# A long-convolution block on one core: the 16-point transforms as 32x32 blocks, and mirrored filter rows in one matmul

## The chip, the cores and the metric

The kernel runs on one core of a Trainium2 chip. The metric is device time in microseconds of one execution. The median of three runs of the kernel before is 1267.15 us.

## The reference

A block with a hyena branch and a pooling branch, for one sequence of L = 2048 positions and 1024 channels. The part that the change touches is the convolution of the 512 hyena channels with filters as long as the sequence, through Fourier transforms, twice over (`HYENA_ORDER` = 2).

```python
def hyena_filters(L, w1, b1, w2, b2, w3, b3, freq, w_proj):
    ...
    h = (h @ w_proj).reshape(L, HYENA_ORDER, N_DIRECTIONS, HYENA_WIDTH)
    ...
    return h * decay[:, None, None, :]

def two_sided_spectrum(h):
    ...
    k_full = jnp.concatenate([k_fwd, jnp.zeros_like(k_fwd[:1]), k_bwd[:0:-1]], axis=0)
    return jnp.fft.rfft(k_full, n=2 * L, axis=0)

def fft_conv(u, k_f, d):
    ...
    u_f = jnp.fft.rfft(uf, n=2 * L, axis=1)
    y = jnp.fft.irfft(u_f * k_f[None], n=2 * L, axis=1)[:, :L]
    return (y + uf * d.astype(jnp.float32)).astype(u.dtype)

def hybrid_layer(x, ...):
    h = rms_norm(x, pre_g)
    p = jnp.einsum('bld,dk->blk', h, w_in)
    hy = short_conv(p[..., :HYENA_IN], conv_w, conv_b)
    v = hy[..., :HYENA_WIDTH]
    gates = (hy[..., HYENA_WIDTH:2 * HYENA_WIDTH], hy[..., 2 * HYENA_WIDTH:])
    ...
    k_f = two_sided_spectrum(hyena_filters(L, ...))
    y = v
    for o in range(HYENA_ORDER):
        y = gates[o] * fft_conv(y, k_f[:, o], hyena_d[o])
    y_h = rms_norm(y * jax.nn.silu(z_h), norm_h_g)
    y_p = rms_norm(multiscale_pool(u_p, pool_w, pool_scale) * jax.nn.silu(z_p), norm_p_g)
    out = jnp.einsum('blk,kd->bld', jnp.concatenate([y_h, y_p], axis=-1), w_out)
    return x + rms_norm(out, post_g)
```

## The kernel before

**Stages.** From 0 to 404 us of the span the input projection and the pooling branch run, from 404 to 599 us the projection in natural layout (L553 to L555), from 599 to 644 us the head of the convolution phase, from 644 to 1120 us eight loops `gloop(o, q)` (o is the order 0 or 1, q one of four blocks of 128 channels), and from 1120 to 1264 us the tail with the output projection.

**The transform.** A sequence of 2048 points is transformed in two stages: 128-point transforms over the partitions (`s1` for the signal, `s1k` for the filter, with the tables f1 and f1s), a rearrangement by 32x32 transposes on DVE (`trans`, L623), and 16-point transforms in `gloop`. The transformed signal lies in BS[q], the transformed filter in BK[o, q]; both are f32.

**A gloop** has eight steps m. `kern(m)` (L720 to L725) transforms the filter by four f32 matmuls of 128x128 against `gf`, a table with four blocks on the diagonal of each 128x128 square; ACT copies the two halves of the partitions to kk (L722, L723), and two DMAs on SP's queue write them again to the other half, since the complex product needs each value on both halves. `mult(m)` (L732 to L739) transforms the signal by four matmuls against `gf`; ACT makes the swapped copy xs (L734, L735), DVE multiplies the product px by kk (L737), POOL multiplies xs by kk (L738), DVE adds both (L739). `back(m)` (L746, L747) transforms back by four matmuls against `gi`, and ACT copies the result to BS[q]. The order of the closures is kern(m+1), mult(m), back(m-1). pk, px and pc have a PSUM bank each (tags pk, x, c, one buffer each); f has a bank, k and s two each.

**Order of the work.** `run(main, *sides)` mixes the closures of side lists among those of a gloop by their place in the list: the filter of a later gloop (`pre_k`: `gen` makes filter rows, `s1k` transforms them), the signal of a later gloop (`post0`, `post1`, `pre_s`) and tiles of the output projection of the pooling branch (`fills`, L815 to L838). The calls of `run`, first `gloop(0, 0)`, then (0, 1), (1, 0), (1, 1), (0, 2), (0, 3), (1, 2), (1, 3), stand in L849 to L875. The framework orders the instructions of each engine from there and sets the waits; each engine executes in that order. `gen(j)` has two halves h, each with two rows n2 and for each the two directions dr: eight matmuls of 128 columns in f32r (L669), the high and the low part of the weights in turn.

## Time and profile before

| | us |
|---|---|
| median of three runs (1261.64 to 1273.34) | 1267.15 |
| profiled execution, its own time | 1265.96 |
| its span | 1264.0 |
| head of the convolution phase, 599 to 644 | 45.0 |
| eight gloops, 644 to 1120, 64 steps | 476.0 |
| tail, 1120 to 1264 | 144.0 |

PE is TensorE's matmuls, PEld its weight loads, DVE VectorE, ACT ScalarE, POOL GpSimd, SP SyncE. Busy times are shares of a stretch; a matmul's end is modelled. An f32 matmul shows as two rows of PE and two of PEld, so a count of 512 stands for 256 matmuls of the program. A row of a timeline gives start, length, engine, line, operation, tiles out<-in, shape, and in brackets the idle time before it with what ended it.

### The profile page before, as it was taken

The numbers are of one execution on the slowest core, as the hardware profiler recorded it, in microseconds if no ns is written. First come the engines' busy times: TensorE is split into PE (matmuls) and PEld (weight loads), VectorE is DVE, ScalarE is ACT, GpSimd is POOL, SyncE is SP. The second block draws the span as 40 slices with busy tenths as digits, with TensorE's granted clock in tenths as the row PEclk, the third lists the DMA queues.
The fourth block names the chain that finished last, engine by engine and source line by source line (L and its number), as shares of the span: only waits on it lengthen the run. The fifth ranks groups of instructions, "written<-read, shape, count | busy, mean of one in ns | idle before, by whom it ended". The sixth has DMA issues, their size and how long they took to land. (4 is left out here: it accounts for less than half of the span.)

```text
span 1264.0 us, 19047 instructions
## 1 busy us (share of the span) xinstructions
PE 1174.8 (93%) x7064; PEld 1012.7 (80%) x7064; DVE 823.8 (65%) x1343; ACT 480.5 (38%) x795; POOL 488.4 (39%) x436
## 2 busy tenths in 40 slices
PE   7999999999999999899899899999998999899984
PEld 5788888787788999899677788887887888877763
DVE  6965538436536658566464777766567777658987
ACT  7612112111112111200236566655556666844221
POOL 3212021504452568557222445422325354334534
PEclk9899999999999999999899999999999999999987
DMA  7224122223242253423795435456564447465574
GB/s 256 86 59 126 35 84 83 84 78 113 90 146 79 86 152 97 134 77 138 266 309 167 129 111 141 137 179 200 151 182 127 122 131 215 141 199 167 202 257 142
DMA packets 112950, 179.49 MB, mean 142 GB/s; under 512 B 11337, under 2 KB 60249, under 8 KB 111577
## 3 DMA queue, kind: packets, MB, share of 16 engines
q1 hardware_dynamic: 111032, 175.30, 44.9%
q10 hardware_dynamic: 1648, 2.44, 0.6%
q8 instruction: 56, 0.92, 0.3%
q0 software_dynamic: 176, 0.53, 0.1%
q14 instruction: 38, 0.30, 0.1%
HBM read 114.80 MB, written 45.61 MB: 127 GB/s over the span
## 5 line engine op out<-in xcount | busy, mean ns | idle before, releaser
L738 POOL TENSOR_TENSOR xs<-xs,kk 128x512 f32<-128x512 f32 x64 | 82.2, 1284 | 217.7 <-ACT xs L735 202.0
L553 PE MATMUL nm<-wh,XH 128*128 128x256 f32 x512 | 145.7, 285 | 6.9 <-DVE a L560 6.1
L555 PE MATMUL nm<-wh,XL 128*128 128x256 f32 x512 | 145.4, 284 | 0.0
L554 PE MATMUL nm<-wl,XH 128*128 128x256 f32 x512 | 145.1, 283 | 0.0
L560 DVE SCALAR_TENSOR_TENSOR a<-nm,r_nat,wc 128x256 f32<-128x256 f32 x192 | 81.5, 474 | 51.0 <-DMA a0p<-a 12.6
L553 PEld LDWEIGHTS nm<-wh,XH 128*128 128x128 f32 x512 | 97.7, 191 | 7.6 <-DVE a L560 6.8
L320 PE MATMUL mm<-XH,wh 128*128 128x512 f32 x256 | 103.0, 402 | 0.0
L322 PE MATMUL mm<-XH,wl 128*128 128x512 f32 x256 | 102.2, 399 | 0.0
L321 PE MATMUL mm<-XL,wh 128*128 128x512 f32 x256 | 101.5, 396 | 0.0
L554 PEld LDWEIGHTS nm<-wl,XH 128*128 128x128 f32 x512 | 97.8, 191 | 0.0
L555 PEld LDWEIGHTS nm<-wh,XL 128*128 128x128 f32 x512 | 97.5, 190 | 0.0
L623 DVE STREAM_TRANSPOSE BS<-BS 128x1024 f32<-128x1024 f32 x64 | 76.5, 1221 | 14.0 <-ACT BS L747 14.0
L732 PE MATMUL px<-BS,gf 128*128 128x128 f32 x512 | 73.6, 281 | 5.2 <-DVE yt L737 5.2
L737 DVE TENSOR_TENSOR yt<-px,kk 128x512 f32<-128x512 f32 x64 | 43.5, 680 | 52.8 <-ACT xs L735 49.2
L746 PE MATMUL pc<-yt,gi 128*128 128x128 f32 x512 | 69.4, 278 | 9.1 <-DVE yt L739 9.1
L674 POOL TENSOR_TENSOR sd<-ab 128x512 f32<-128x512 f32 x32 | 52.4, 1636 | 62.8 <-DVE ab L670 62.7
L746 PEld LDWEIGHTS pc<-yt,gi 128*128 128x128 f32 x512 | 63.4, 191 | 16.0 <-ACT kk L722 8.3
L732 PEld LDWEIGHTS px<-BS,gf 128*128 128x128 f32 x512 | 66.0, 190 | 12.1 <-DVE yt L737 7.7
L720 PE MATMUL pk<-BK,gf 128*128 128x128 f32 x512 | 69.3, 276 | 1.3 <-ACT kk L723 1.3
L682 PE MATMUL s1k<-sd,f 128*128 128x512 f32 x128 | 64.1, 619 | 6.2 <-DVE ab L670 2.8
L720 PEld LDWEIGHTS pk<-BK,gf 128*128 128x128 f32 x512 | 64.3, 188 | 6.5 <-issue 4.3
L739 DVE TENSOR_TENSOR yt<-yt,xs 128x512 f32<-128x512 f32 x64 | 55.3, 864 | 20.2 <-POOL xs L738 19.8
(213 smaller groups left out, 3210.0 us busy)
## 6 DMA issues: line engine op xcount, KB each, us to landing
fy<-yp_d SPq DMA_DIRECT2D x32, 512.0 KB
kk<-kk SPq DMA_DIRECT2D x128, 128.0 KB
dec<-t_dec SPq DMA_DIRECT2D x30, 512.0 KB
wr<-w SPq DMA_DIRECT2D x16, 512.0 KB
ut<-v_d SPq DMA_DIRECT2D x32, 256.0 KB
op_d<-fo SPq DMA_DIRECT2D x32, 256.0 KB
gt<-g_d SPq DMA_DIRECT2D x32, 256.0 KB
o<-op_d SPq DMA_DIRECT2D x32, 256.0 KB
```

The lines of the kernel that those rows point to most:

```text
L320: T.matmul(ps, wh, XH[lb][:, d], start=(d == 0), stop=False)
L321: T.matmul(ps, wh, XL[lb][:, d], start=False, stop=False)
L322: T.matmul(ps, wl, XH[lb][:, d], start=False, stop=(d == NT - 1))
L553: T.matmul(ps, xh[:, d, ls], wh, start=(d == 0), stop=False)
L554: T.matmul(ps, xh[:, d, ls], wl, start=False, stop=False)
L555: T.matmul(ps, xl[:, d, ls], wh, start=False, stop=(d == NT - 1))
L560: V.scalar_tensor_tensor(out=a[s], in0=ps, scalar=r_nat[:, l2:l2 + 1], in1=wc[:, s], op0=ALU.mult, op1=ALU.mult)
L623: V.transpose(out=ap, in_=ap)
L720: T.matmul(pk[:, k], gf[:, 4 * m + k], BK[o, q][:, 2 * m + k // 2, :, k % 2], start=True, stop=True)
L732: T.matmul(px[:, k], gf[:, 4 * m + k], BS[q][:, 2 * m + k // 2, :, k % 2], start=True, stop=True)
L738: G.tensor_tensor(out=xs, in0=xs, in1=kk[:, 1], op=ALU.mult)
L746: ins = T.matmul(pc[:, k // 2, k % 2], gi[:, 4 * m + k], yt[:, k], start=True, stop=True)
```

## The change

The 128x128 tables with four diagonal blocks become blocks of 32x32. A matmul in `kern`, `mult` and `back` takes 32 partitions of data and 32 columns of weights and writes 32 partitions of PSUM, so that there are 16 positions on the array; the list `order` visits them diagonally. `gx` and `gk` have two blocks for each position: one gives real and imaginary parts, the other the swapped and signed (gx) or doubled (gk) ones. `kern` is 32 matmuls and one ACT copy of 128x1024, without the DMAs; `mult` is 32 matmuls, one DVE multiply of 128x1024 and one POOL add of the two halves; `back` is 16 matmuls and the ACT copy. All three write one PSUM tile `PB` of four banks, each bank with four slots of 128 columns: slots 0 and 1 for mult, 2 and 3 for kern, and slot 2 again for back. The order of the closures becomes back(m-1), kern(m+1), mult(m).

The rows n and 16-n of the filter are made next to each other (`ROWS`), and share their two left operands: a matmul of `gen` has 256 columns, and a half has four in place of eight (six where row 0 is in it). Both copies of `s1k` go to ACT. In `post0` a step is cut into `split`, `gate` and `s1`, each one closure later than the one before. The PSUM tag f joins k. The tables loaded at the head are 2.6 MB in place of 4.2 MB. In the tail the output matmuls use PB's banks, `pg` is loaded into the place of gi after the last gloop, and one of four y buffers is used twice.

```diff
...
+        re = np.concatenate([c, s], axis=1).transpose(1, 0, 2)
+        im = np.concatenate([-s, c], axis=1).transpose(1, 0, 2)
+        q = slice(j * 32, j * 32 + 32)
+        gx[q, :, 0] = np.concatenate([re, im], axis=2)
+        gx[q, :, 1] = np.concatenate([-im, re], axis=2)
...
-    gf = fp.tile([P, 32, P], F32, tag="gf", name="gf")
-    gi = fp.tile([P, 32, P], F32, tag="gi", name="gi")
+    gx = fp.tile([P, 32, 2, 32], F32, tag="gx", name="gx")
+    gk = fp.tile([P, 32, 2, 32], F32, tag="gk", name="gk")
+    gi = fp.tile([P, 8, 4, 32], F32, tag="gi", name="gi")
     fwp = pool(ph2, "fwp")
     psB = pool(ph2, "psB", 1, PS)
+
+    PB = psB.tile([P, 4, 4, P], F32, name="PB")
...
-            wh = hp.tile([P, 256], F32R, tag="kwh", name=f"kwh{u}", bufs=2)
-            wl = hp.tile([P, 256], F32R, tag="kwl", name=f"kwl{u}", bufs=2)
-            S.copy(out=wh, in_=wr)
-            V.tensor_tensor(out=wl, in0=wr, in1=wh, op=ALU.subtract)
+            wh = abp.tile([P, 384], F32R, tag="kwh", name=f"kwh{u}", bufs=2)
+            wl = abp.tile([P, 384], F32R, tag="kwl", name=f"kwl{u}", bufs=2)
+            for a, b in ((0, 256), (256, 384)):
+                S.copy(out=wh[:, a:b], in_=wr[:, 0:b - a])
+                V.tensor_tensor(out=wl[:, a:b], in0=wr[:, 0:b - a], in1=wh[:, a:b], op=ALU.subtract)
...
                 ps = psB.tile([P, 2, 2, P], F32, tag="k", name=f"gen{u}_{j}_{h}", bufs=2)
-                for i in range(2):
-                    n2 = 4 * j + 2 * h + i
-                    for dr in range(2):
-                        c0 = n2 if dr == 0 else 16 - n2
-                        lh = HT[:, c0 % R, c0 // R:c0 // R + 128]
-                        for k_, wt in enumerate(st_["w"]):
-                            T.matmul(ps[:, i, dr], lh, wt[:, dr * P:dr * P + P], start=(k_ == 0), stop=(k_ == 1))
+
+                n = ROWS[4 * j + 2 * h]
+                psf = ps.rearrange("p a b c -> p (a b) c")
+                if n:
+                    todo = [(n, psf[:, 0:4:3], 0, 2), (16 - n, psf[:, 1:3], 1, 3)]
+                else:
+                    todo = [(0, psf[:, 0], 0, 1), (16, psf[:, 1], 1, 2), (8, psf[:, 2:4], 0, 2)]
+                for c0, o_, a, b in todo:
+                    lh = HT[:, c0 % R, c0 // R:c0 // R + 128]
+                    for k_, wt in enumerate(st_["w"]):
+                        T.matmul(o_, lh, wt[:, a * P:b * P], start=(k_ == 0), stop=(k_ == 1))
...
-                (V.tensor_copy if ri else S.copy)(out=dst, in_=ps)
+                S.copy(out=dst, in_=ps)
...
         kks, yts = {}, {}
+        order = [(j, (j + d) % 4) for d in range(4) for j in range(4)]
+
+        def fwd(B, tab, m, slot):
+            for k in range(2):
+                for j, i in order:
+                    js = slice(32 * j, 32 * j + 32)
+                    ins = T.matmul(PB[32 * i:32 * i + 32, j, slot + k], tab[js, 4 * m + i, k],
+                                   B[js, 2 * m + i // 2, :, i % 2], start=True, stop=True)
+            return ins
 
         def kern(m):
-            pk = psB.tile([P, 4, P], F32, tag="pk", name=f"pk{u}_{m}", bufs=1)
-            for k in range(4):
-                T.matmul(pk[:, k], gf[:, 4 * m + k], BK[o, q][:, 2 * m + k // 2, :, k % 2], start=True, stop=True)
-            kk = wp.tile([P, 2, 4, P], F32, tag="kk", name=f"kk{u}_{m}", bufs=2)
-            S.copy(out=kk[0:64, 0], in_=pk[0:64])
-            S.copy(out=kk[64:128, 1], in_=pk[64:128])
-            Q.dma_start(out=kk[64:128, 0], in_=kk[0:64, 0])
-            Q.dma_start(out=kk[0:64, 1], in_=kk[64:128, 1])
+            fwd(BK[o, q], gk, m, 2)
+            kk = wp.tile([P, 4, 2, P], F32, tag="kk", name=f"kk{u}_{m}", bufs=2)
+            S.copy(out=kk, in_=PB[:, :, 2:4])
             kks[m] = kk
 
         def mult(m):
-            kk = kks.pop(m)
-            px = psB.tile([P, 4, P], F32, tag="x", name=f"px{u}_{m}", bufs=1)
-            for k in range(4):
-                T.matmul(px[:, k], gf[:, 4 * m + k], BS[q][:, 2 * m + k // 2, :, k % 2], start=True, stop=True)
-            xs = fp.tile([P, 4, P], F32, tag="xs", name=f"xs{u}_{m}", bufs=2)
-            S.mul(out=xs[0:64], in_=px[64:128], mul=-1.0)
-            S.copy(out=xs[64:128], in_=px[0:64])
-            yt = fp.tile([P, 4, P], F32, tag="yt", name=f"yt{u}_{m}", bufs=3)
-            V.tensor_tensor(out=yt, in0=px, in1=kk[:, 0], op=ALU.mult)
-            G.tensor_tensor(out=xs, in0=xs, in1=kk[:, 1], op=ALU.mult)
-            V.tensor_tensor(out=yt, in0=yt, in1=xs, op=ALU.add)
+            fwd(BS[q], gx, m, 0)
+            yt = fp.tile([P, 4, 2, P], F32, tag="yt", name=f"yt{u}_{m}", bufs=3)
+            V.tensor_tensor(out=yt, in0=PB[:, :, 0:2], in1=kks.pop(m), op=ALU.mult)
+            G.tensor_tensor(out=yt[:, :, 0], in0=yt[:, :, 0], in1=yt[:, :, 1], op=ALU.add)
             yts[m] = yt
 
         def back(m):
             yt = yts.pop(m)
-            pc = psB.tile([P, 2, 2, P], F32, tag="c", name=f"pc{u}_{m}", bufs=1)
-            for k in range(4):
-                ins = T.matmul(pc[:, k // 2, k % 2], gi[:, 4 * m + k], yt[:, k], start=True, stop=True)
-            S.copy(out=BS[q][:, 2 * m:2 * m + 2].rearrange("p a c i -> p a i c"), in_=pc)
+            for i, j in order:
+                js = slice(32 * i, 32 * i + 32)
+                ins = T.matmul(PB[32 * j:32 * j + 32, i, 2], gi[js, m, j], yt[js, j, 0], start=True, stop=True)
+            S.copy(out=BS[q][:, 2 * m:2 * m + 2].rearrange("p a c i -> p a i c"),
+                   in_=PB[:, :, 2].rearrange("p (a i) c -> p a i c", i=2))
             if after:
                 after(m, ins)
 
         r = [lambda: kern(0)]
         for m in range(8):
+            if m:
+                r.append(lambda m=m: back(m - 1))
             if m + 1 < 8:
                 r.append(lambda m=m: kern(m + 1))
             r.append(lambda m=m: mult(m))
-            if m:
-                r.append(lambda m=m: back(m - 1))
...
-        ps = psB.tile([P, 512], F32, tag="f", name=f"fp{k}", bufs=1)
+        ps = psB.tile([P, 512], F32, tag="k", name=f"fp{k}", bufs=2)
...
-        for t_, n_ in ((gf, "t_gf"), (gi, "t_gi")):
-            for a in range(0, 32, 8):
-                Q.dma_start(out=t_[:, a:a + 8], in_=I[n_][:, a:a + 8])
+        for t_, n_ in ((gk, "t_gk"), (gx, "t_gx"), (gi, "t_gi")):
+            n = t_.shape[1] // 2
+            for a in range(2):
+                Q.dma_start(out=t_[:, a * n:a * n + n], in_=I[n_][:, a * n:a * n + n])
...
-    yb2 = fp.tile([P, 2, 4, 512], F32R, tag="gi", name="yb2")
-    O1 = fp.tile([P, 2, 4, 512], F32R, tag="gf", name="O1")
+    pg = fp.tile([P, D], F32, tag="gi", name="pg")
+    Q.dma_start(out=pg, in_=I["pg"].broadcast_to([P, D]))
+    O1 = [fp.tile([P, 4, 512], F32R, tag=t_, name=f"O1{t_}") for t_ in ("gx", "gk")]
...
-                ps = psB.tile([P, 512], F32, tag=(("x", "pk")[i % 2], "k")[dh], name=f"po{l2}_{dh}", bufs=1 + dh)
+                ps = PB[:, 2 * (i % 2) + dh].rearrange("p s c -> p (s c)")
```

The first place is TensorE's order near the end of `gloop(0, 1)`: PB is the shared PSUM tile, pk, px and pc the three separate ones, a name's digits are o, q and the step. Before:

```order
L720 MATMUL pk01_7_6697<-BK01_5647,gf_5265 128x128 [waits PE_49,Activation_49]
L720 MATMUL pk01_7_6697<-BK01_5647,gf_5265 128x128 x3
L732 MATMUL px01_6_6709<-BS1_5913,gf_5265 128x128 [waits DVE_49]
L732 MATMUL px01_6_6709<-BS1_5913,gf_5265 128x128 x3
L746 MATMUL pc01_5_6722<-yt01_5_6667,gi_5266 128x128 [waits DVE_49,Activation_49]
L746 MATMUL pc01_5_6722<-yt01_5_6667,gi_5266 128x128 x3
L720 MATMUL pk10_0_6754<-BK10_6184,gf_5265 128x128 [waits PE_49,Activation_49]
```

Now, back(5), kern(7) and mult(6) of the same loop:

```order
L756 MATMUL PB_5274<-yt01_5_7399,gi_5267 32x128 [waits Pool_49]
L756 MATMUL PB_5274<-yt01_5_7399,gi_5267 32x128 x15
...
L735 MATMUL PB_5274<-BK01_5669,gk_5266 32x128 [waits Activation_49]
L735 MATMUL PB_5274<-BK01_5669,gk_5266 32x128 x31
...
L735 MATMUL PB_5274<-BS1_6102,gx_5265 32x128 [waits Activation_49]
L735 MATMUL PB_5274<-BS1_6102,gx_5265 32x128 x31
```

A group of four matmuls became one of 16 or 32, back moved ahead of kern and mult, and each group waits: back for POOL, kern and mult for ACT. The matmuls left out between them are `gen` and other side work.

The second place is ScalarE's order around the same steps. Before, it makes two copies for kern (L722, L723), two for mult (L734, L735) and one for back (L747):

```order
L722 COPY kk01_7_6702<-pk01_7_6697 64x512 [waits DMAHW1_49,DVE_49,DMAHW2_49,PE_49,Pool_49]
L723 COPY kk01_7_6702<-pk01_7_6697 64x512
L734 ACTIVATE xs01_6_6714<-px01_6_6709 64x512 [waits PE_49,Activation_49]
L735 COPY xs01_6_6714<-px01_6_6709 64x512
L747 COPY BS1_5913<-pc01_5_6722 128x2x2x128 [waits PE_49]
```

Now it makes one for back (L757) and one for kern (L742), with side work between:

```order
L757 COPY BS1_6102<-PB_5274 128x2x2x128 [waits DVE_49,PE_49]
L742 COPY kk01_6_7346<-PB_5274 128x1024 [waits PE_49,Activation_49]
L659 CAST kwh02_8685<-kw02_8681 128x256 [waits DMAHW2_49,DMAHW0_49]
L659 CAST kwh02_8685<-kw02_8681 128x128
L757 COPY BS1_6102<-PB_5274 128x2x2x128 [waits DVE_49,PE_49]
L857 ACTIVATE fo12_7774<-fp12_7761,rpn_75 128x512 [waits PE_49]
L742 COPY kk01_7_7488<-PB_5274 128x1024 [waits PE_49,Activation_49]
```

Three copies a step left ACT's order, and the copy for kern now stands behind the copy for back of the step before in a fixed turn.

The third place is a half of `gen` on TensorE (kwh and kwl are the two parts of the weights, HT the left operand). Before:

```order
L669 MATMUL gen10_1_0_6256<-kwh10_6157,HT_2774 128x128 [waits DVE_49]
L669 MATMUL gen10_1_0_6256<-kwl10_6158,HT_2774 128x128
L669 MATMUL gen10_1_0_6256<-kwh10_6157,HT_2774 128x128
L669 MATMUL gen10_1_0_6256<-kwl10_6158,HT_2774 128x128
L669 MATMUL gen10_1_0_6256<-kwh10_6157,HT_2774 128x128
L669 MATMUL gen10_1_0_6256<-kwl10_6158,HT_2774 128x128
L669 MATMUL gen10_1_0_6256<-kwh10_6157,HT_2774 128x128
L669 MATMUL gen10_1_0_6256<-kwl10_6158,HT_2774 128x128
```

Now, the same half for the next channels:

```order
L836 MATMUL fp12_7761<-fh0_5321,fy12_7759 128x512
L681 MATMUL gen11_1_0_7817<-kwh11_7637,HT_2774 128x2x128 [waits PE_49]
L681 MATMUL gen11_1_0_7817<-kwl11_7638,HT_2774 128x2x128
L681 MATMUL gen11_1_0_7817<-kwh11_7637,HT_2774 128x256
L681 MATMUL gen11_1_0_7817<-kwl11_7638,HT_2774 128x256
```

Behind the last matmul of a tile of `fills` (fp12), eight matmuls of 128 columns became four of 256.

## Rows read from the trace of the kernel before

**Rows 1.** Page, part 1: busy time, share of the span, instructions of each engine

```profile
PE 1174.8 (93%) x7064; PEld 1012.7 (80%) x7064; DVE 823.8 (65%) x1343; ACT 480.5 (38%) x795; POOL 488.4 (39%) x436
```

**Rows 2.** Windows: head, gloops, tail; columns as the first row names them

```profile
core 0: us, PE busy (x) PEld busy (x) DVE busy (x) ACT busy (x) POOL busy (x), PEclk, DMA share, GB/s
599.00:644.00 45.00, 38.12 (x194) 29.19 (x193) 21.70 (x28) 13.29 (x22) 9.42 (x9) 0.89 0.82 290
644.00:1120.00 476.00, 443.78 (x3098) 390.26 (x3098) 325.27 (x417) 296.60 (x510) 184.55 (x135) 0.99 0.55 159
```

**Rows 3.** Lines in 644:1120: busy us, mean ns | idle before, releaser

```profile
L732 PE MATMUL px<-BS,gf 128*128 128x128 f32 x512 | 73.6, 281 | 5.2 <-DVE yt L737 5.2
L746 PE MATMUL pc<-yt,gi 128*128 128x128 f32 x512 | 69.4, 278 | 9.1 <-DVE yt L739 9.1
L720 PE MATMUL pk<-BK,gf 128*128 128x128 f32 x512 | 69.3, 276 | 1.3 <-ACT kk L723 1.3
L669 PE MATMUL gen<-kwh,HT 128*128 128x128 f32 x221 | 51.9, 277 | 0.0
```

**Rows 4.** Timeline in 763:769, two successive steps of one gloop

```profile
763.80 1.17 PE L732 MATMUL px<-BS,gf 128*128 128x128 f32 x8 [0.26 <-DVE yt L737]
764.41 0.69 DVE L739 TENSOR_TENSOR yt<-yt,xs 128x512 f32<-128x512 f32 x1 [0.67 <-POOL xs L738]
...
765.22 0.97 PEld L746 LDWEIGHTS pc<-yt,gi 128*128 128x128 f32 x8 [0.44 <-ACT kk L722]
...
766.22 0.58 ACT L735 COPY xs<-px 64x512 f32<-64x512 f32 x1
...
766.88 1.27 POOL L738 TENSOR_TENSOR xs<-xs,kk 128x512 f32<-128x512 f32 x1 [2.50 <-ACT xs L735]
...
767.58 0.95 PE L732 MATMUL px<-BS,gf 128*128 128x128 f32 x6 [0.23 <-DVE yt L737]
```

**Rows 5.** Timeline in 700:722 and 1136:1138, matmuls and weight loads

```profile
700.28 0.98 PEld L732 LDWEIGHTS px<-BS,gf 128*128 128x128 f32 x8 [0.34 <-DVE yt L737]
...
703.50 0.19 PEld L669 LDWEIGHTS gen<-kwl,HT 128*128 128x128 f32 x1
...
705.50 1.13 PE L746 MATMUL pc<-yt,gi 128*128 128x128 f32 x8 [0.50 <-DVE yt L739]
...
706.67 0.61 ACT L747 COPY BS<-pc 128x512 f32<-128x512 f32 x1 [0.82 <-PE pc L746]
...
717.90 1.88 PE L682 MATMUL s1k<-sd,f 128*128 128x512 f32 x4
...
1136.79 0.97 PEld L914 LDWEIGHTS yss<-one,ya 128*128 128x128 f32 x8
```

**Rows 6.** Lines, shapes apart, whole run: the nearest rows to the new operations

```profile
L239 ACT CAST wh<-wr 128x1024 fp32r<-128x1024 f32 x16 | 16.8, 1049 | 47.6 <-PE mm L321 27.5 <-DMA wr<-w 19.6 <-DVE HT L520 0.5
L293 DVE TENSOR_TENSOR xr<-xr 128x1024 f32<-128x1024 f32 x4 | 5.0, 1254 | 3.4 <-ACT xr L292 3.4
L674 POOL TENSOR_TENSOR sd<-ab 128x512 f32<-128x512 f32 x32 | 52.4, 1636 | 62.8 <-DVE ab L670 62.7
```

**Rows 7.** Lines in 644:1120, shapes apart: operations that the change removes, moves or keeps

```profile
L738 POOL TENSOR_TENSOR xs<-xs,kk 128x512 f32<-128x512 f32 x64 | 82.2, 1284 | 217.7 <-ACT xs L735 202.0 <-DMA kk<-kk 8.5 <-issue 7.1
L739 DVE TENSOR_TENSOR yt<-yt,xs 128x512 f32<-128x512 f32 x64 | 55.3, 864 | 20.2 <-POOL xs L738 19.8
L737 DVE TENSOR_TENSOR yt<-px,kk 128x512 f32<-128x512 f32 x64 | 43.5, 680 | 52.8 <-ACT xs L735 49.2 <-DMA kk<-kk 1.8 <-PE gen L669 0.5
L747 ACT COPY BS<-pc 128x512 f32<-128x512 f32 x63 | 39.5, 628 | 21.6 <-PE pc L746 20.8
...
L722 ACT COPY kk<-pk 64x512 f32<-64x512 f32 x64 | 36.9, 577 | 34.5 <-POOL xs L738 20.9 <-PE pk L720 12.1 <-DVE yt L739 0.5
...
L684 DVE COPY BK<-s1k 128x512 f32<-128x512 f32 x28 | 19.2, 686 | 17.0 <-PE s1k L682 16.8
```

More of the change, by code (lines that the diff above doesn't have):

```diff
@@ L51, in _tables @@
     g = np.arange(32)
-    gf = np.zeros((32, 128, 128))
-    gi = np.zeros((32, 128, 128))
+    gx = np.zeros((128, 32, 2, 32))
+    gk = np.zeros((128, 32, 2, 32))
+    gi = np.zeros((4, 32, 8, 4, 32))
     n2 = np.arange(16)
     k2 = np.arange(16)
+    rows = np.array(ROWS)
     for j in range(4):
@@ L89, in _tables @@
     dt = np.concatenate([dt, sh], axis=1)
-    n2 = np.arange(16)
+    n2 = np.array(ROWS)
     dt = np.stack([dt[:, n2], dt[:, 16 - n2]], axis=2)
@@ L761, in post0 @@
     def post0(q):
-        uts, gts = {}, {}
-        def step(m):
-            if m < 8:
-                if m % 2 == 0:
-                    gts[m // 2] = fp.tile([P, 4, P], F32, tag="gt", name=f"gt0{q}_{m}", bufs=2)
-                    Q.dma_start(out=gts[m // 2], in_=g0_d[q // 2][:, 2 * m:2 * m + 4, (q % 2) * P:(q % 2) * P + P])
-                dd = wp.tile([P, 2, 2, 2, P], F32R, tag="dd", name=f"dd{q}_{m}", bufs=2)
-                src = rows(q)[:, :, m].rearrange("p r c i -> p r i c")
-                S.copy(out=dd[:, 0], in_=src)
-                G.tensor_tensor(out=dd[:, 1], in0=src, in1=dd[:, 0], op=ALU.subtract)
-                ps = psB.tile([P, 2, P], F32, tag="s", name=f"py0{q}_{m}", bufs=2)
-                for ri in range(2):
-                    mm3(ps, 2 + ri, dd[:, 0, ri], dd[:, 1, ri], ri == 0, ri == 1)
-                g_ = gts[m // 2][:, 2 * (m % 2):2 * (m % 2) + 2]
-                V.tensor_tensor(out=g_, in0=ps, in1=g_, op=ALU.mult)
-                ut = abp.tile([P, 2, 2, P], F32R, tag="ut", name=f"ut1{q}_{m}", bufs=3)
-                S.copy(out=ut[:, 0], in_=g_)
-                V.tensor_tensor(out=ut[:, 1], in0=g_, in1=ut[:, 0], op=ALU.subtract)
-                uts[m] = ut
-            if m:
-                s1(q, "1", m - 1, uts.pop(m - 1))
@@ L785, in post0, with split @@
-        return ([lambda cb=cb: trans(BS[q], cb) for cb in range(4)] + [lambda m=m: step(m) for m in range(9)]
-                + [lambda cb=cb: trans(BS[q], cb) for cb in range(4)])
+        uts, gts, dds = {}, {}, {}
+        def split(m):
+            if m % 2 == 0:
+                gts[m // 2] = fp.tile([P, 4, P], F32, tag="gt", name=f"gt0{q}_{m}", bufs=2)
+                Q.dma_start(out=gts[m // 2], in_=g0_d[q // 2][:, 2 * m:2 * m + 4, (q % 2) * P:(q % 2) * P + P])
+            dd = wp.tile([P, 2, 2, 2, P], F32R, tag="dd", name=f"dd{q}_{m}", bufs=2)
+            src = rows(q)[:, :, m].rearrange("p r c i -> p r i c")
+            S.copy(out=dd[:, 0], in_=src)
+            G.tensor_tensor(out=dd[:, 1], in0=src, in1=dd[:, 0], op=ALU.subtract)
+            dds[m] = dd
@@ new lines, in gate @@
+        def gate(m):
+            dd = dds.pop(m)
+            ps = psB.tile([P, 2, P], F32, tag="s", name=f"py0{q}_{m}", bufs=2)
+            for ri in range(2):
+                mm3(ps, 2 + ri, dd[:, 0, ri], dd[:, 1, ri], ri == 0, ri == 1)
+            g_ = gts[m // 2][:, 2 * (m % 2):2 * (m % 2) + 2]
+            V.tensor_tensor(out=g_, in0=ps, in1=g_, op=ALU.mult)
+            ut = abp.tile([P, 2, 2, P], F32R, tag="ut", name=f"ut1{q}_{m}", bufs=3)
+            S.copy(out=ut[:, 0], in_=g_)
+            V.tensor_tensor(out=ut[:, 1], in0=g_, in1=ut[:, 0], op=ALU.subtract)
+            uts[m] = ut
@@ L788, in py1 @@
+        r = [lambda cb=cb: trans(BS[q], cb) for cb in range(4)]
+        for m in range(10):
+            if m < 8:
+                r.append(lambda m=m: split(m))
+            if 0 < m < 9:
+                r.append(lambda m=m: gate(m - 1))
+            if m > 1:
+                r.append(lambda m=m: s1(q, "1", m - 2, uts.pop(m - 2)))
+        return r + [lambda cb=cb: trans(BS[q], cb) for cb in range(4)]
     def py1(q, lb):
@@ L862, in build @@
     op = pool(ost, "op", 1, None, "right")
-    pg = op.tile([P, D], F32, name="pg")
-    Q.dma_start(out=pg, in_=I["pg"].broadcast_to([P, D]))
     O0 = op.tile([P, 2, 4, 512], F32R, name="O0")
@@ L900, in split_y @@
             if cb == 2:
[L901 removed]
+                gt = fp.tile([P, 512], F32, tag="yc", name=f"yc{lb}", bufs=2)
                 Q.dma_start(out=gt, in_=y_d[2][:, ls])
@@ L911, in stat_y @@
     def stat_y(lb, ya):
-        ss = psB.tile([P, 4], F32, tag="f", name=f"yss{lb}", bufs=1)
+        ss = psB.tile([P, 4], F32, tag="k", name=f"yss{lb}", bufs=2)
         for i in range(4):
```

30 lines of the change are left out of this document (12 added, 18 removed).

## The prediction

> **What bounds the kernel now.** The page's busy shares come first: PE 93%, DVE 65%, the others under 40% [rows 1]. A share over the whole span says little about one stage, so the windows by stage come next. The gloops take 476.0 of the 1264.0 us, 476/64 = 7.44 us a step, with PE busy for 443.8 us (93%), DVE 325.3, ACT 296.6 and POOL 184.6, at a granted clock of 0.99 [rows 2]. So PE sets the pace there. The three transforms hold it for 73.6 + 69.4 + 69.3 = 212.3 us [rows 3], and each pass works mostly on zeros, since three of four blocks of the tables are empty.
>
> Then the timeline of a stretch without much side work. There a step takes 767.58 - 763.80 = 3.78 us [rows 4]: kern, mult and back have banks of their own, so the next px starts as soon as DVE has read the last one, while pc and the copy behind it run beside it. The other half of the 7.44 us is side work on a busy PE. The long idle time ahead of POOL (217.7 us, 202.0 of it behind ACT's xs [rows 7]) and ahead of DVE's product (52.8) is time off the bound: these engines wait for PE's turn.
>
> **The chain after the change.** With one PSUM tile for all three, the order printed in the section on the change shows the waits: back waits for POOL, kern for ACT's copy of that back (slot 2 is used by both), mult for ACT's copy of kk, DVE for mult, POOL for DVE. A step is then one chain without overlap, kern, ACT, mult, DVE, POOL, back, ACT, and the next kern stands behind its end. PE falls to 443.8 - 212.3 = 231.5 us, less some 25 from gen, plus the small matmuls, and ceases to be the bound if these are quick. The question is whether the chain is shorter than 7.44 us.
>
> *Matmul groups.* A pass of 128 f32 columns streams in 0.107 us: four passes of 512 columns take 1.88 us, less 0.17 for the last one's way out is 1.71, over 16 pieces of 128 [rows 5]. That 0.17 is the length of one pass, 0.278 [rows 3], less 0.107. Start to start is a little more, (0.98 - 0.19)/7 = 0.113 for eight loads [rows 5]. A group of 32 small f32 matmuls is 64 passes. No row shows sixteen blocks at once. If sixteen stream fully side by side, T = 64 x 0.107/16 = 0.43 us. If nothing overlaps, 64 x 0.113 = 7.2 us. I take T = 0.63: the floor, and half of what a start costs beyond streaming (0.006 x 64 = 0.38, half 0.2) left uncovered. It is nearer to the floor since successive passes lie on different rows and columns of the array but for the two of one matmul. With the way out, a group of 32 takes 0.80, back with 16 takes 0.49.
>
> The Trainium skill, "TensorE: Matmul & The Clock Gate", section "Measured speedup vs the span model", gives 10.6 times for sixteen 32x32 tiles with 512 columns; by it T would be about 64 x 0.107/10.6 = 0.65, an estimate, and the forecast would stand. No row here shows it.
>
> *The other operations.* ACT's copy of 128x1024 takes 1.05 (the cast of that shape; twice the PSUM copy of 128x512, 0.63, would be 1.26). DVE's product takes 1.25 (128x1024 add; twice L737 is 1.36). POOL's add of two strided halves takes 1.64, as L674, which reads halves of a tile in the same stride; L738, unstrided, has 1.28, and is the lower bound [rows 6, 7]. The copy to BS stays 0.63. Hand-overs: PE to ACT 0.04 (705.50 + 1.13 to 706.67 [rows 5]), DVE to PE 0.12 (764.41 + 0.69 to 765.22), ACT to POOL 0.08 (766.22 + 0.58 to 766.80, start 766.88) [rows 4]. I take 0.12 into PE and 0.08 into POOL from every engine.
>
> *The sum of a step.* kern 0.80 + 0.04 + ACT 1.05 + 0.12 = 2.01. mult 0.80 + 0.04 + DVE 1.25 + 0.08 = 2.17. POOL 1.64 + 0.12 = 1.76. back 0.49 + 0.04 + ACT 0.63 + 0.12 = 1.28. Together 7.22 us, and 6.72 with T = 0.43.
>
> *Waits behind side work.* The chain's operations stand in a fixed order with the side work. DVE keeps 325.3 - 55.3 (L739) - 43.5 (L737) - 19.2 (L684, which moves to ACT) = 207 us of it, 3.2 a step. ACT keeps 296.6 less five groups from 39.5 to 36.9 us (together 188.6) plus L684's 28 copies at 0.63, 126 us, 2.0 a step. POOL keeps 184.6 - 82.2 = 102, 1.6 a step. PE keeps 231.5 - 25, 3.2 a step [rows 2, 3, 7]. As shares of 7.2 us that is 0.44, 0.28, 0.22 and 0.44. The chain visits DVE and POOL once, ACT twice and PE three times: 2.5 meetings a step if they fell at random, each costing half an operation of about 0.6 us, 0.76 us. The order puts much of the side work where the chain is elsewhere, so I take 0.5, with 0.2 and 1.0 as ends. A step is 7.72 us, 64 steps 494 us, against 476: +18. Queued behind a waiting group on PE are gen, s1k and fills; they have room (206 + 64 x 2.1 = 340 of 494 us), so their own delay costs nothing unless a gloop ends on them.
>
> *The rest.* The 128 kk transfers leave SP's queue; they released POOL for 8.5 of its 217.7 idle us [rows 7], so I count nothing. gen's halves go from eight passes to four of twice the columns: some 443 passes at 0.113 (50 us) to about 210 at less than twice that, perhaps 25 us of PE. Before, that is on the bound; after, PE has slack, and it counts nothing. If PE were still the bound this would be the gain. The extra 128 columns of weights cost two short copies for each of eight filters, off the path. In the head 1.6 MB less is loaded, at 290 GB/s 5.4 us with DMA busy 0.82 and PE 38.1 of 45 us [rows 2]; I take -4 of 0 to -5.4. The tail's new banks and buffers I take at 0, with 0 to +5 since pg is loaded after the last gloop and one y buffer is used twice.
>
> 1265.96 + 18 - 4 = **1280 us** against the profiled execution, which lies 1.2 us under the median. The likeliest case's own range, by the ends of the waits: 7.42 x 64 = 475 gives 1261, 8.22 x 64 = 526 gives 1312.
>
> **The rivals.**
>
> *Faster: the chain is shorter than a PE-bound step.* With T = 0.43, POOL at L738's 1.28 and waits of 0.3, a step is 6.72 - 0.36 + 0.3 = 6.66, 64 of them 426 us: 1265.96 - 50 - 4 = 1212. It decides below about 7.3 us a step (467 us, 1253). For it: PE loses its load, every side engine has room, and all three assumptions are the lower ends of rows. Against it: L674's stride is that of the new add, and a chain in fixed order with this much side work seldom waits so little.
>
> *Weight loads are the limit.* Every pass has its own load. Eight passes with a single streamed column each (L914) still take (0.97 - 0.19)/7 = 0.111 each [rows 5], so the load of 128 columns takes about that; 32 columns in proportion 0.028. If loads follow one another, T = 64 x 0.028 = 1.8, a step 7.72 + 2.5 x 1.17 = 10.6, 681 us: 1467. For it: before, loads are in order and evenly spaced. Against it: the loads of different blocks may go side by side.
>
> *The two passes of one matmul wait for each other.* An f32 matmul is two passes on one block. If passes start in order, and the second must wait until the first has streamed, then every matmul costs 0.107, whatever the other 15 blocks do: T = 32 x 0.107 = 3.4, a step 7.72 + 2.5 x 2.8 = 14.7, 940 us: 1726. For it: the passes of before start strictly in turn, 0.113 apart. Against it: there all passes share the whole array, so the rows can't tell. The Trainium skill, "TensorE: Matmul & The Clock Gate", section "Part 3: Packing small matmuls — row/col tiling", states that matmuls start and end strictly in program order; taken together with two passes per block this speaks against the change. The rows of before agree with an order in turn.
>
> **How the numbers follow.** Likeliest case 0.36, faster 0.30, loads 0.16, paired passes 0.18. About 1%, 1254 to 1280, is what a measurement of this kernel can tell from no change. The faster rival gives 0.30 and the low corner of the likeliest case 0.01; just under half of the likeliest case lies within 1% (0.17); its rest and both slow rivals give 0.52. The range runs from 1195, a little under the faster rival, to 1480, above the loads, and leaves the paired passes (0.18) out.
>
> **What would show it.** In the changed kernel's trace: the length of a group of 32 small matmuls (0.80 right; 2 or 3.6 for the slow rivals); POOL's add at 1.64 or 1.28; PE's idle time ahead of back released by POOL, ahead of kern and mult by ACT, a step with no two of its operations beside each other; PE's share in the gloops well under 93%. Wrong it would be if kern and mult overlapped with the step before, if gloops ended on side work, or if PE's granted clock, 0.99 now, fell as PE idles, since every pass would then stream at half the pace.

## The result

The changed kernel takes 1401.63 us, median of 4 runs (1396.2 to 1406.32), beside 1270.11 us for the kernel before in the same runs. The ratio is 1.1045, with a 95% interval from 1.0973 to 1.1117: 10% slower. The profiled execution has a span of 1404.1 us, 140 more than before.

Page of the changed kernel, part 1, and its windows over head, gloops and tail (columns as in [rows 2]); the first answers [rows 1], the others [rows 2], whose tail has no row there and follows as the last line, from the kernel before:

```profile
PE 1204.8 (86%) x15528; PEld 938.8 (67%) x15528; DVE 775.3 (55%) x1255; ACT 416.8 (30%) x643; POOL 484.6 (35%) x436
```

```profile
599.00:645.00 46.00, 37.15 (x161) 27.00 (x159) 18.74 (x25) 16.71 (x27) 9.83 (x9) 0.85 0.87 291
645.00:1241.00 596.00, 466.22 (x11579) 315.41 (x11579) 293.88 (x334) 233.37 (x357) 183.40 (x137) 0.87 0.32 100
1241.00:1404.00 163.00, 123.57 (x527) 96.38 (x525) 100.56 (x275) 37.09 (x86) 54.74 (x28) 0.93 0.52 168
```

```profile
1120.00:1264.00 144.00, 114.49 (x519) 92.67 (x518) 114.89 (x277) 41.24 (x92) 57.70 (x30) 0.91 0.57 191
```

The gloops went from 476 to 596 us (+120), the tail from 144 to 163 (+19), the head from 45 to 46. That is the whole of the 140. In the gloops PE's busy share fell from 93% to 78%, no engine is near full, and the granted clock fell from 0.99 to 0.87. A step takes 596/64 = 9.31 us in place of 7.44. Lines of the three groups in the gloops of the changed kernel (mult, kern, back):

```profile
L735 PE MATMUL PB<-BS,gx 32*32 32x128 f32 x4096 | 77.5, 317 | 12.7 <-ACT kk L742 10.8 <-ACT BS L757 1.7
L735 PE MATMUL PB<-BK,gk 32*32 32x128 f32 x4096 | 75.7, 309 | 11.7 <-ACT BS L757 10.1 <-ACT kk L742 1.1 <-issue 0.3
L756 PE MATMUL PB<-yt,gi 32*32 32x128 f32 x2048 | 35.3, 303 | 78.3 <-POOL yt L749 78.3
```

Back waits for POOL, kern and mult for ACT. The groups take 77.5 + 75.7 + 35.3 = 188.5 us, where the three transforms took 212.3 before [rows 3]. TensorE's share fell, but its busy time in the gloops did not: it rose from 443.8 to 466.2 us.

A step with little in its way, timeline of the changed kernel (PE, ACT, DVE and POOL of the chain; side work left out):

```profile
897.26 0.51 PE L756 MATMUL PB<-yt,gi 32*32 32x128 f32 x32 [0.45 <-POOL yt L749]
...
897.95 0.63 ACT L757 COPY BS<-PB 128x512 f32<-128x512 f32 x1 [4.74 <-PE PB L756]
...
898.63 1.10 PE L735 MATMUL PB<-BK,gk 32*32 32x128 f32 x64
...
899.83 1.02 ACT L742 COPY kk<-PB 128x1024 f32<-128x1024 f32 x1 [0.51 <-PE PB L735]
...
901.03 1.09 PE L735 MATMUL PB<-BS,gx 32*32 32x128 f32 x64
...
902.26 1.23 DVE L748 TENSOR_TENSOR yt<-PB,kk 128x1024 f32<-128x1024 f32 x1 [3.60 <-PE PB L735]
...
903.57 1.28 POOL L749 TENSOR_TENSOR yt<-yt 128x512 f32<-128x512 f32 x1 [6.36 <-DVE yt L748]
...
904.90 0.51 PE L756 MATMUL PB<-yt,gi 32*32 32x128 f32 x32 [0.58 <-POOL yt L749]
```

No two of these seven lie beside each other: back, ACT, kern, ACT, mult, DVE, POOL, back again after 904.90 - 897.26 = 7.64 us. This already is longer than the 7.44 us of a step before. The other 9.31 - 7.64 = 1.67 us a step, 107 us in all, is what comes between. A long step shows it, timeline of TensorE and of two operations of DVE in the changed kernel:

```profile
669.23 1.09 PE L735 MATMUL PB<-BK,gk 32*32 32x128 f32 x64
670.25 1.98 PE L694 MATMUL s1k<-sd,f 128*128 128x512 f32 x4
672.08 0.50 PE L834 MATMUL fp<-fh,fy 128*128 128x512 f32 x1
...
672.93 4.63 DVE L630 STREAM_TRANSPOSE BK<-BK 128x1024 f32<-128x1024 f32 x4 [5.55 <-ACT BK L696]
...
674.75 0.40 PE L836 MATMUL fp<-fh,fy 128*128 128x512 f32 x1
675.08 1.09 PE L735 MATMUL PB<-BS,gx 32*32 32x128 f32 x64
...
677.48 1.19 DVE L748 TENSOR_TENSOR yt<-PB,kk 128x1024 f32<-128x1024 f32 x1
...
680.06 0.51 PE L756 MATMUL PB<-yt,gi 32*32 32x128 f32 x32 [1.47 <-POOL yt L749]
```

In the clean step mult starts 2.40 us after kern. Here it starts 5.85 us after, since four passes of s1k and twelve of fills stand between them in TensorE's order, with no idle time. Behind mult fourteen more stand ahead of back, and then PE idles 1.47 us for POOL, which is late since DVE's product stood behind four transposes, 4.63 us in one piece. The step takes 13.2 us: side work and chain take turns, on TensorE's queue and on DVE's.

The same comparison over all 64 steps, each leg of the chain against the same leg of the clean step, divides the 107 us by the engine at which the leg ends: 42 us at TensorE, 30 at DVE, 21 at ACT, 14 at POOL. At the other three engines the chain loses more than at TensorE. Part of what ends at ACT and DVE is groups that ran longer at the lower clock; the experiment on the clock has its size.

### The profile page after: what moved, and what is told of

The parts are those of the page before. It is cut to its first block, busy times and chain, and to the rows that moved or that the text cites. A ratio compares the mean times of both kernels' runs of the same rounds, so it can differ in the third digit from the quotient of the medians.

```text
span 1404.1 us, 35240 instructions
## 1 busy us (share of the span) xinstructions
PE 1204.8 (86%) x15528; PEld 938.8 (67%) x15528; DVE 775.3 (55%) x1255; ACT 416.8 (30%) x643; POOL 484.6 (35%) x436
## 5 line engine op out<-in xcount | busy, mean ns | idle before, releaser
L749 POOL TENSOR_TENSOR yt<-yt 128x512 f32<-128x512 f32 x64 | 82.3, 1286 | 260.7 <-DVE yt L748 258.1
L748 DVE TENSOR_TENSOR yt<-PB,kk 128x1024 f32<-128x1024 f32 x64 | 78.0, 1219 | 121.3 <-PE PB L735 121.0
L756 PE MATMUL PB<-yt,gi 32*32 32x128 f32 x2048 | 35.3, 303 | 78.3 <-POOL yt L749 78.3
L735 PE MATMUL PB<-BS,gx 32*32 32x128 f32 x4096 | 77.5, 317 | 12.7 <-ACT kk L742 10.8
L735 PE MATMUL PB<-BK,gk 32*32 32x128 f32 x4096 | 75.7, 309 | 11.7 <-ACT BS L757 10.1
L756 PEld LDWEIGHTS PB<-yt,gi 32*32 32x32 f32 x2048 | 16.1, 108 | 102.1 <-POOL yt L749 101.6
L757 ACT COPY BS<-PB 128x512 f32<-128x512 f32 x64 | 39.8, 622 | 148.8 <-PE PB L756 148.8
L742 ACT COPY kk<-PB 128x1024 f32<-128x1024 f32 x64 | 64.8, 1012 | 59.5 <-PE PB L735 59.2
L735 PEld LDWEIGHTS PB<-BS,gx 32*32 32x32 f32 x4096 | 49.9, 112 | 43.9 <-ACT kk L742 18.4
L735 PEld LDWEIGHTS PB<-BK,gk 32*32 32x32 f32 x4096 | 48.8, 109 | 39.7 <-ACT BS L757 23.5
```

Source lines behind the costliest of these rows:

```text
L735: ins = T.matmul(PB[32 * i:32 * i + 32, j, slot + k], tab[js, 4 * m + i, k], B[js, 2 * m + i // 2, :, i % 2], start=True, stop=True)
L742: S.copy(out=kk, in_=PB[:, :, 2:4])
L748: V.tensor_tensor(out=yt, in0=PB[:, :, 0:2], in1=kks.pop(m), op=ALU.mult)
L749: G.tensor_tensor(out=yt[:, :, 0], in0=yt[:, :, 0], in1=yt[:, :, 1], op=ALU.add)
```

## The experiments

The theory after the result: **A**, the shared PSUM tile makes a step one chain, and this chain and what stands in it set the time. Rivals: **B**, PE is still the bound, through more passes and switches of tile size; **C**, the lower clock. The tail is a question of its own.

**The gen part alone, on the kernel before.** L669's eight matmuls become the four of the changed kernel.

```diff
-                for i in range(2):
-                    n2 = 4 * j + 2 * h + i
-                    for dr in range(2):
...
-                            T.matmul(ps[:, i, dr], lh, wt[:, dr * P:dr * P + P], start=(k_ == 0), stop=(k_ == 1))
+                for c0, o_, a, b in todo:
...
+                        T.matmul(o_, lh, wt[:, a * P:b * P], start=(k_ == 0), stop=(k_ == 1))
```

> The kernel before with one part of the change alone: mirrored filter rows share their matmuls (four of 256 columns for eight of 128). The table of kern is not permuted with the rows, so the filter's rows stand in another order than the reference wants; the amount of work is that of the real thing. Theory A (PE sets the pace of the gloops of before, 93% busy): PE loses about 25 us of passes and the gloops get 15 to 25 us shorter, about 1245. Rival (the chain of a step sets it, PE is only busy beside it): within 5 us of 1267.

1250.75 us, ratio 0.9853 (0.9829 to 0.9876): the part that is not about small blocks gains 19 us (15 between the profiled executions). Windows from the first matmul of kern to the last copy into BS, of the kernel before and of this one:

```profile
644.10:1120.80 476.70, 444.48 (x3100) 390.82 (x3100) 325.17 (x418) 297.16 (x512) 184.55 (x135) 0.99 0.55 159
```

```profile
638.80:1105.50 466.70, 428.54 (x2896) 370.83 (x2897) 337.90 (x426) 299.62 (x520) 179.68 (x135) 0.99 0.57 167
```

With 16 us less of PE's busy time the gloops are 10 us shorter, less than the 15 to 25 expected; the head, where gen runs too, is 5 us shorter. On a kernel where PE sets the pace, PE time is worth most of its length.

**Side work first.** `run` gives out all side closures, then the gloop.

```diff
-        for e in sorted(ev, key=lambda e: e[:3]):
-            e[3]()
+        for sd in sides + (main,):
+            for f in sd:
+                f()
```

> The changed kernel with run() giving out the side closures ahead of the gloop, not mixed in, so that most steps of the gloop run without side work. The whole gets longer under either theory, since less lies beside each other; the reading is the period of a step in the clean stretches. Theory A (one chain through the shared PSUM tile, and waits behind side work on top): 7.4 to 7.8 us a step without side work, against a mean of 9.3 in the changed kernel, so the waits cost some 1.6 us a step, 100 us. Rival (the chain alone is as long as the mean, side work costs nothing): about 9 us a step in clean stretches.

1613.7 us, a single run. The period without side work is 8.5 us, neither of the two. The window over three such steps and TensorE's timeline in one of them, and the window of the changed kernel's clean step:

```profile
713.30:738.70 25.40, 11.21 (x496) 6.57 (x480) 3.67 (x3) 4.86 (x6) 3.78 (x3) 0.50 0.01 3
```

```profile
721.22 0.74 PE L754 MATMUL PB<-yt,gi 32*32 32x128 f32 x32 [2.73 <-POOL yt L747]
722.79 1.53 PE L733 MATMUL PB<-BK,gk 32*32 32x128 f32 x64 [0.83 <-ACT BS L755]
725.48 1.52 PE L733 MATMUL PB<-BS,gx 32*32 32x128 f32 x64 [1.16 <-ACT kk L740]
```

```profile
897.30:904.90 7.60, 7.02 (x188) 5.34 (x189) 1.92 (x2) 4.08 (x6) 1.28 (x1) 1.00 0.73 215
```

With nothing but the chain, PE is busy for 11.21 of 25.4 us, the granted clock is 0.50, the lower of its two levels, and groups take 1.53 and 0.74 us in place of 1.09 and 0.51. In the clean step, with side work around the chain, PE is busy for 7.02 of 7.60 us and the granted clock is 1.00, the higher level. So the chain alone is 8.5 us at the lower clock and 7.64 at the higher. My expectation of 7.4 to 7.8 us left out that the clock would fall with the side work gone.

**back behind mult**, as in the kernel before.

```diff
-            if m:
-                r.append(lambda m=m: back(m - 1))
             if m + 1 < 8:
                 r.append(lambda m=m: kern(m + 1))
             r.append(lambda m=m: mult(m))
+            if m:
+                r.append(lambda m=m: back(m - 1))
```

> The changed kernel with the order of closures of before, kern(m+1), mult(m), back(m-1), so that back no longer follows the POOL add of the same step. Theory A (one chain sets the pace): POOL's 1.29 us and its two hand-overs (0.31 and 0.12) lie beside kern and ACT's copy, 1.4 to 1.7 us less a step, 90 to 110 us less, about 1300. Rival B (PE is the bound, 466 of 596 us busy with the switches between tile sizes): no PE work is taken away, 1395 to 1405.

1354.48 us, ratio to before 1.0679 (1.0646 to 1.0712): 47 less than the changed kernel with the same work on every engine. That speaks for A and against B. Half of what was expected came. One of the shortest steps, from kern to kern:

```profile
807.92 1.08 PE L735 MATMUL PB<-BK,gk 32*32 32x128 f32 x64
...
814.36 1.09 PE L735 MATMUL PB<-BK,gk 32*32 32x128 f32 x64
```

It takes 6.44 us in place of 7.64, which would be 77 us in 64 steps, and the gloops took 542 us in place of 596: 54 less. What comes between rose from 1.67 to 542/64 - 6.44 = 2.03 us a step.

**kern and mult in one burst.** Both groups first, then ACT's copy and DVE's product, then back(m-1).

```diff
         def mult(m):
+            if m + 1 < 8:
+                kern(m + 1)
             fwd(BS[q], gx, m, 0)
+            if m + 1 < 8:
+                kcopy(m + 1)
```

> The changed kernel with kern(m+1) and mult(m) issued back to back, ACT's copy of kern and DVE's product behind both, and back(m-1) behind these. Same work on every engine. Theory A (one chain sets the pace): kern's copy and DVE's product lie beside each other, POOL beside PE; a step alone is 2.3 + 0.1 + 1.2 + 0.2 + 0.6 + 0.1 + 0.6 + 0.2 = 5.3 us, with 1.6 of waits 6.9, 440 us for 64 steps in place of 596, about 1245. Rival B (PE is the bound): 1385 to 1405.

1343.89 us, ratio 1.0588 (1.0554 to 1.0622). 58 us less, where 155 were expected. Lines of its gloops:

```profile
L754 DVE TENSOR_TENSOR yt<-PB,kk 128x1024 f32<-128x1024 f32 x64 | 77.8, 1216 | 111.1 <-ACT kk L744 104.2 <-PE PB L735 6.7
```

```profile
788.90 0.98 PE L735 MATMUL PB<-BK,gk 32*32 32x128 f32 x56
...
794.75 0.99 PE L735 MATMUL PB<-BK,gk 32*32 32x128 f32 x56
```

DVE's product waits for ACT's copy (104.2 us), not for TensorE: two readers of the same four banks come one after the other as well, so the two operations that I had put beside each other stayed in the chain. The shortest full step is 794.75 - 788.90 = 5.85 us where 5.3 was put. But the gloops took 530 us, 8.28 a step, so what comes between is now 2.43 us. In the three orders the chain alone is 7.64, 6.44 and 5.85 us, and what comes between 1.67, 2.03 and 2.43: the side work is the same, and part of what a shorter chain gives goes into longer waits behind it.

**Half the passes.** Only the first of the two tables; the products lack their second half.

```diff
-            for k in range(2):
+            for k in range(1):
```

> The changed kernel with the first of the two tables only: kern and mult are 16 matmuls each in place of 32. This leaves the swapped operands out, so the products lack their second half. Theory (a group costs by the number of its passes, 64 x 0.0127 us from first to last load, and some 0.38 to the reader): the two groups take 0.79 each in place of 1.19, 0.8 us less a step, 50 us less, about 1350. Rival (a group costs a fixed time, for the switch of the array and the way out): 1390 to 1400.

1337.33 us, a single run; PB is also set to zero once at its start. The line of kern in its gloops (that of the changed kernel stands in the result, 75.7 us):

```profile
L736 PE MATMUL PB<-BK,gk 32*32 32x128 f32 x2048 | 35.7, 308 | 16.7 <-ACT BS L758 13.9 <-ACT kk L743 2.7
```

A group of 32 passes takes 35.7/64 = 0.56 us, one of 64 takes 75.7/64 = 1.18. Two groups of 0.62 less in 64 steps are 79 us, and the gloops took 525 in place of 596, 71 less. The group's length comes from its passes, and what the groups lose the step loses nearly in full.

**Blocks row by row.**

```diff
-        order = [(j, (j + d) % 4) for d in range(4) for j in range(4)]
+        order = [(j, i) for j in range(4) for i in range(4)]
```

> The changed kernel with the 16 blocks of a group visited row by row (the four blocks with the same 32 partitions of data one after the other) in place of diagonally. Theory (passes of different blocks start 0.0127 us apart in any order): groups of 64 passes stay at 1.09 us, 1395 to 1405. Rival (blocks that share data partitions wait for each other, a pass streaming 0.107 us): four blocks of a row hold the next row up, groups of 1.7 us or more, at least 64 x 2.5 x 0.6 = 96 us longer, 1500 or over.

1402.76 us, a single run: the same as the diagonal order. Blocks that share their data partitions don't hold each other up by an amount that the time shows; the rival asked for 1500 or over.

**gen undone in the changed kernel.**

```diff
-                for c0, o_, a, b in todo:
...
+                            T.matmul(ps[:, i, dr], lh, wt[:, dr * P:dr * P + P], start=(k_ == 0), stop=(k_ == 1))
```

> The changed kernel with gen undone: eight matmuls of 128 columns a half again, in the new order of rows. Theory A (in the changed kernel a chain sets the pace and PE has room): the 25 us of passes come back beside the chain and cost 0 to 8 us, 1400 to 1410. Rival B (PE is still near its bound there): 15 to 25 us, 1417 to 1427.

1441.02 us, ratio 1.1357 (1.1337 to 1.1377): 39 us more than the changed kernel (33 between the profiled executions), more than either expected. Its gloops, from the first matmul of kern to the last copy into BS:

```profile
648.00:1275.80 627.80, 497.03 (x11792) 347.83 (x11792) 297.70 (x334) 234.00 (x358) 183.67 (x137) 0.86 0.30 93
```

PE is busy for 31 us more and the gloops are 32 us longer, though PE idles 131 of 628 us. So A as I had put it, with PE's side work beside the chain for nothing, is wrong: PE isn't full, and its time still costs its full length. The long step above shows how: a group of the chain can't pass the side work ahead of it in TensorE's order, and that side work can't fill the gap behind when the order has put none there. By legs, 26 of the 32 us lie between kern's copy and mult. In the last gloop, where no gen runs, the steps of both kernels are alike (8.5 us).

**Tiles of its own for the tail.** Four PSUM tiles of one bank in place of PB's four.

```diff
-                ps = PB[:, 2 * (i % 2) + dh].rearrange("p s c -> p (s c)")
+                ps = psT.tile([P, 512], F32, tag=f"t{i % 2}{dh}", name=f"po{l2}_{dh}", bufs=1)
```

> The changed kernel with four PSUM tiles of one bank for the tail's output matmuls in place of the four banks of PB; the rest stays. Theory (the tail's 163 us against 143 before come from waits on PB as a whole: TensorE waits for DVE's last read of it, 1.6 to 2.0 us in each of 16 steps): tail 140 to 150, 1380 to 1390. Rival (the tail is longer for what was moved behind the last gloop: pg, the second half of the output weights, the y buffer used twice): tail 158 to 163, 1395 to 1405.

1385.4 us, ratio 1.0923 (1.0875 to 1.097): 16 us less. In the changed kernel's timeline of TensorE and DVE in the tail

```profile
1342.40 0.39 PE L836 MATMUL PB<-O1gx,yb 128*128 128x512 f32 x1
...
1342.89 1.41 DVE L965 SCALAR_TENSOR_TENSOR o<-PB,rr,o 128x512 f32<-128x512 f32 x2 [1.69 <-PE PB L836]
...
1344.36 0.50 PE L834 MATMUL PB<-O,yb 128*128 128x512 f32 x1 [1.57 <-DVE o L965]
```

TensorE idles 1.57 us while DVE reads banks that the next matmuls don't write: the wait that the framework sets there is on PB as a whole. With tiles of their own, the tail is 147 us (last copy to BS at 1235.3, span 1382.4).

**Burst and tail tiles together.**

```diff
+            if m + 1 < 8:
+                kern(m + 1)
...
+                ps = psT.tile([P, 512], F32, tag=f"t{i % 2}{dh}", name=f"po{l2}_{dh}", bufs=1)
```

> The changed kernel with kern(m+1) and mult(m) issued back to back, and with four PSUM tiles of their own for the tail's output matmuls. Theory (two waits on the shared PSUM tile, in two stages, that add up): the 58 us of the first and the 16 to 19 of the second, 1325 to 1330, still behind the kernel before. Rival (the tail's gain is eaten since the shorter gloops push their side work into the tail): 1335 to 1345.

1327.18 us, ratio 1.0482 (1.0432 to 1.0533). The two gains add up (58 + 16), and it is still 5% behind the kernel before.

**The clock.** 32 groups of eight matmuls that nobody reads, beside the last two gloops.

```diff
-    run(gloop(1, 2), post0(3), pre_k(1, 3), fills(24, 28))
+    run(gloop(1, 2), post0(3), pre_k(1, 3), fills(24, 28), [lambda k=k: warm(k) for k in range(16)])
```

> The changed kernel with 32 groups of eight matmuls of 512 columns whose result nobody reads, given out as side work beside the last two gloops (7.4 us of TensorE's time for each four groups). Theory C (the lower granted clock in the last gloop, 0.59, is due to TensorE's idle time, and costs there): the clock of these gloops rises above 0.9, back's group takes 0.51 in place of 0.74, and the last two gloops, 151 us, get 5 to 15 us shorter although 60 us of work is added; about 1392. Rival (the clock costs nothing there, or the added work stands in the chain's way): 151 us or more.

1417.51 us, a single run. Windows of the last two gloops, each from its first matmul of kern, of the changed kernel and of this one:

```profile
1086.50:1162.60 76.10, 49.80 (x1421) 33.30 (x1421) 38.10 (x44) 34.75 (x55) 26.12 (x19) 0.85 0.30 96
1162.60:1240.90 78.30, 39.76 (x1346) 27.29 (x1347) 20.50 (x19) 18.50 (x24) 16.15 (x12) 0.59 0.17 55
```

```profile
1085.50:1179.80 94.30, 84.07 (x1566) 60.06 (x1565) 45.42 (x48) 37.16 (x57) 29.50 (x21) 0.96 0.27 89
1179.80:1251.70 71.90, 60.42 (x1456) 42.51 (x1456) 20.56 (x19) 18.49 (x24) 16.77 (x12) 0.94 0.18 60
```

In the last gloop the clock rose from 0.59 to 0.94, the clean steps went from 8.5 to 7.8 us, and with 21 us more of PE's busy time the gloop got 6 us shorter. So the lower clock does cost, some 0.7 us a step there. But in the gloop before it the added passes stood in the chain, 94 us in place of 76, and the whole became longer. C is a part of the loss. Over all gloops the chain's groups take 188.5 us where 64 x (1.09 + 1.09 + 0.51) = 172 would be their time at the higher clock: some 16 of the 120 us. What the side work lost at the lower clock no run separates.

**A version that beats both.** The kernel before, with shared matmuls in gen; s1k's copy is split in two so that each row goes to its natural place and kern's table stays.

```diff
-                dst = BK[o, q][:, ri * 8 + 2 * j:ri * 8 + 2 * j + 2].rearrange("p a c i -> p a i c")
-                (V.tensor_copy if ri else S.copy)(out=dst, in_=ps)
+                for x in range(2):
+                    n0, n1 = sorted(ROWS[4 * j + 2 * x:4 * j + 2 * x + 2])
+                    a0, a1 = ri * 8 + n0 // 2, ri * 8 + n1 // 2
+                    (V.tensor_copy if ri else S.copy)(out=BK[o, q][:, a0:a1 + 1:a1 - a0, :, n0 % 2], in_=ps[:, x])
```

> The kernel before with the shared matmuls of mirrored filter rows, and s1k's copy out of PSUM split into two of 128x256, so that each row lands at its natural place and kern's table stays as it is. Theory A (PE sets the pace of before; ACT and DVE have room): the 19 us of the run with shared rows alone stay, less a little for 64 more short copies on engines that are not the bound: 1248 to 1256. Rival (ACT and DVE stand on the path there too): the copies cost 64 x 0.17 = 11 us and more, 1260 or over.

1249.87 us, ratio 0.9852 (0.9819 to 0.9886). Its gloops, between the same two places as above:

```profile
636.90:1105.00 468.10, 430.29 (x2896) 372.89 (x2897) 340.88 (x454) 301.16 (x548) 178.81 (x135) 0.99 0.57 166
```

PE lost 14 us of busy time there and the gloops 9, and they start 7 us earlier; DVE gained 16 and is at 73%.

**The same with the changed kernel's post0** (split, gate and s1 one closure apart).

```diff
+            if 0 < m < 9:
+                r.append(lambda m=m: gate(m - 1))
+            if m > 1:
+                r.append(lambda m=m: s1(q, "1", m - 2, uts.pop(m - 2)))
```

> The kernel before with shared matmuls of mirrored rows (natural row places) and with the changed kernel's post0: split, gate and s1 as closures one step apart. Theory (PE is the bound, 422 of 457 us busy, and some of its 35 us of idle time are waits inside post0): 0 to 8 us less than 1249.9. Rival (the lag moves s1 and the transposes behind it later, toward the end of the gloop): 0 to 8 us more.

1254.53 us, ratio 0.9888 (0.9857 to 0.9918); its interval overlaps that of the version without it. No gain of this part is seen.

## Why the prediction was right, and where it was not

Slower was forecast, 1280 us with a range from 1195 to 1480; 1401.63 lies in the range and far from the point. The likeliest case's own range ended at 1312: the result is inside only since the range left room for the weight loads, which did not come, and that is luck. The direction is not. The mechanism held: the step is one chain through PB, PE is no longer full, back waits for POOL, kern and mult for ACT, and that chain is not shorter than the 7.44 us of a step before.

*The chain's own length* was 7.22 us as predicted and 7.64 as measured. By legs of the clean step: kern and its copy 2.40 (901.03 - 898.63) for 2.01, mult and DVE 2.54 for 2.17, POOL 1.33 for 1.76, back and its copy 1.37 for 1.28. The groups were undersized: from the first pass to the reader 1.20 and 1.23 us where 0.84 was put. POOL's add was oversized: 1.28, as the contiguous L738 [rows 7], not as L674 [rows 6], though the stride is the same. Together 0.42 us, 27 us in 64 steps. The 1.64 of L674 is a mean of two cases, as the kernel before shows:

```profile
712.20 1.28 POOL L674 TENSOR_TENSOR sd<-ab 128x512 f32<-128x512 f32 x1 [0.42 <-DVE ab L670]
713.13 0.90 DVE L675 TENSOR_TENSOR sd<-ab 128x512 f32<-128x512 f32 x1
...
741.70 0.69 DVE L675 TENSOR_TENSOR sd<-ab 128x512 f32<-128x512 f32 x1
741.75 1.79 POOL L674 TENSOR_TENSOR sd<-ab 128x512 f32<-128x512 f32 x1 [2.16 <-DVE ab L670]
```

It is long where DVE's subtraction of the same tile starts beside it, not for its stride.

*The waits behind side work* are the step that failed. Predicted 0.5 us a step with 1.0 as the end, measured 9.31 - 7.64 = 1.67, which is 75 us more than forecast. The prediction let meetings happen at random and half an operation of 0.6 us be lost at each, and said of gen, s1k and fills on PE's queue that "they have room" and "their own delay costs nothing". The undone gen shows the contrary: 31 us of PE work cost 32 us in the gloops. What was missed is that side work stands in long pieces between two operations of the chain: sixteen passes on TensorE (4.8 us) and four transposes on DVE (4.63 us) in the long step. TensorE's side work was also undersized: 466.2 - 188.5 = 278 us, where 206 was put. The lower clock is in this term too.

*The tail* was put at 0 to +5 and is +19. The change let PB, one tile, replace three tags in the output loop, and TensorE waits for DVE in every turn; 16 us of it went with four tiles. The diff showed this line; the prediction looked at the loads there and not at what waits for PB. *The head* brought +1, not -4: the tables are 1.6 MB smaller, but in its window the queues moved 291 GB/s for 46 us, 13.4 MB, where they had moved 290 for 45, 13.1 MB. Other loads took the tables' place.

*gen* was costed at nothing, "if PE were still the bound this would be the gain". It is worth 39 us in the changed kernel and 19 on the kernel before. The condition was right for the second and the claim wrong for the first.

*The rivals.* The faster one needed a step under 7.3 us; the cleanest step is 7.64. The serial loads would have made T 1.8 us and the paired passes 3.4; the groups show 0.81 from the first pass to the last (1.09 less the 0.28 of one pass). The Trainium skill's rule ("TensorE: Matmul & The Clock Gate", section "Part 3: Packing small matmuls — row/col tiling") that matmuls start strictly in program order would have cost that 3.4 us, if the second pass of a block must wait for the first; the measured 0.81 us says that the two together do not hold here. Which of them fails no run shows.

*Open.* No kernel was run in which kern, mult and back have PSUM tiles of their own in the gloops. That the shared tile makes the chain is read from the waits and from the two other orders; in the tail alone a run took the shared tile away. Two parts of the change, the tag f joined to k and ACT's second copy of s1k, were not undone by themselves.
